# Gate and up products: both parts of x behind the weights' first part, as one operand of 512 columns

## The chip, the cores and the metric

The kernel runs on one core of one Trainium2 chip. The metric is device time in microseconds (us); less is better. Engines are called as the profile calls them: PE (TensorE, matmuls), PEld (its weight loads), DVE (VectorE), ACT (ScalarE), POOL (GpSimd), SP (SyncE, which issues most DMAs).

## The reference, cut to what matters

The model is an encoder of two layers over 256 tokens of 1024 channels. Each layer has a feed-forward part, a group of four mixers, and a second feed-forward part, each between two norms. The feed-forward part is what the change touches:

```
def swiglu(h, w_gate, w_up, w_down):
    return (jax.nn.silu(h @ w_gate) * (h @ w_up)) @ w_down
...
    x = x + 0.5 * rms_norm(swiglu(rms_norm(x, g[0]), gate, up, down), g[1])
```

The gate and up weights are 1024 x 2816, the down weights 2816 x 1024, all float32. There are four such parts in all (two per layer).

## The kernel before

A float32 product is made from matmuls on fp32r operands. Each operand is split in two parts, a first part (hi, a rounded copy made by ACT) and a second part (lo, the rest, made by DVE), and three of the four products of parts are summed: `TERMS = ((0, 0), (0, 1), (1, 0))` in line 253.

Weights come through `Stream.next` (lines 229 to 251). It issues one DMA of 512 KB on SP's queue into one of four raw buffers, then ACT copies hi and DVE subtracts lo into buffers of the pools `w4`, `m4` or `k4`. A raw buffer comes free when DVE's subtraction has read it, and only then is its next DMA issued; a hi or lo buffer comes free when the last matmul that reads it is done.

The 2816 hidden channels are 22 blocks of 128. For a block, `block(fb)` (line 400) computes gate and up: the weights' 128 columns are the stationary operand, the 256 tokens of x are the moving one, and k runs over eight pieces of 128 channels. The two sums, of 256 columns each, lie in the two halves of one PSUM bank, `pg`. Gate (u = 0) takes 24 matmuls, then up (u = 1) takes 24. After that ACT applies Silu to the gate half (tile `h`), DVE multiplies it with the up half, and ACT and DVE split the product into `hT`, hi and lo. `rows` (line 419) then multiplies `hT` with the down weights: moving operands of 512 columns, three matmuls for each half of y and token tile, so 12 matmuls for a block's two token tiles.

The main loop of `ffn` runs block(fb + 1) and then rows(fb), so a block's hT is needed one block later. From block 15 on (`NFB - NEPI`) only the first token tile's rows are done in the loop, 6 matmuls in place of 12; the second tile's are kept for the end, where they cover the norm that joins this part to the next. Blocks 20 and 21 follow each other with no rows between. Block 0, and in three of the four parts blocks 1 and 2 too, go through `half_block` by token tile, which the change leaves as it is but for indices; the first part sends 21 blocks through `block`, the others 19 each.

`pg` has the PSUM tag "d", which has two banks (`PD` = 2). Half blocks, the mixers' projections and the norm's transposes of some tiles use the same two banks. With one bank per block, a block's bank is needed again two blocks later.

`norm_t` (line 275) normalises x and transposes it; its inner `part` (line 299) empties each bank of four transposed pieces with one ACT copy (hi) and one DVE subtraction (lo) of 128 x 512. The four tiles of XT hold hi and lo apart, each with four of the eight pieces.

The order of work on each engine isn't written in the code alone: a scheduler of the framework orders the instructions when the program is built, from priorities in order of the program and a model of their durations. On the chip each engine then takes them in that order, and one that waits holds back those behind it.

Of the kernel before, what the change touches and what calls it, by code (L numbers as in the profile page):

```python
# [9 lines left out]
F32 = mybir.dt.float32  # L10
# [76 lines left out]
# column blocks of w_in in the order in which they are used; -1 marks a column that is not there  # L87
# [18 lines left out]
def tile_encoder(ctx: ExitStack, tc: tile.TileContext, x_in, wffn, win, wout, gains, params, idn, cst, rel, out, dbg=None):  # L106
# [55 lines left out]
    def s1(name, shape=(P, S), dt=F32):  # L162
        return sp.tile(list(shape), dt, tag="s1", bufs=3, name=name)
# [39 lines left out]
    def load_small(l):  # L203
        if l == 0:
            nc.sync.dma_start(out=C, in_=cst)
            # log-sigmoid of the retention's decays: forward, backward
            for i in range(DEPTH):
                o, w = _POFF["rl"]
                nc.sync.dma_start(out=lg[:, i, 0:8], in_=params[i][:, o:o + w])
            act(pair, c_("pair"), AF.Copy)  # L210
            lgr, lgt = lg[:, :, 0:8], lg[:, :, 8:16]
            act(lgt, lgr, AF.Abs)
            act(lgt, lgt, AF.Exp, scale=-1.0)
            act(lgt, lgt, AF.Ln, bias=1.0)
            stt(lgr, lgr, 0.0, lgt, ALU.min, ALU.subtract)
        t = par[l] = sp.tile([P, NPAR], F32, tag="par", bufs=1, name=f"par{l}")
        nc.sync.dma_start(out=t, in_=params[l])
        t = dv[l] = sp.tile([P, 30], F32, tag="dv", bufs=2, name=f"dv{l}")
        ts(t[:, 0:8], p_(l, "mu"), -1.0, ALU.mult, 1.0, ALU.add)
        ts(t[:, 8:16], p_(l, "mu"), 0.5, ALU.mult)  # L220
        ts(t[:, 16:24], par[l][:, _POFF["w0"][0]:_POFF["w0"][0] + 8], 0.5, ALU.mult)
        ts(t[:, 24:26], p_(l, "ka"), 0.5, ALU.mult)
        ts(t[:, 26:28], p_(l, "ka"), -0.5, ALU.mult, 1.0, ALU.add)
        ts(t[:, 28:30], p_(l, "kk"), 512.0, ALU.mult)

# [1 line left out]
    @contextmanager  # L227
    def held(*ins):
        """the instructions issue after these, each on its own engine."""
        with ExitStack() as c:  # L230
            for i in ins:
                c.enter_context(tc.issue_after(i.ins))
            yield
# [37 lines left out]
    def new_xt(l, i):  # L271
        new = m4 if i == 2 else k4
        return [[new([P, 4, S], F32R, name=f"XT{l}_{i}{a}{q}") for q in range(2)] for a in range(2)]

    def norm_t(XT, g, tk, tag, hold=()):
        """The normalised x with its gain, transposed, in two parts: [part][k // 4][d, k % 4, token].
        What it returns issues the transposes."""
# [21 lines left out]
        def part(q):  # L299
            pt = ps.tile([P, 4, P], F32, tag=tag, bufs={"d": PD, "a": PA, "y": PY}[tag], name="pt")  # L300
            for k in range(4):
                T.transpose(pt[:, k, :], xg[:, (q * 4 + k) * P:(q * 4 + k + 1) * P], ident)
            hi = XT[0][q][:, :, tk * P:(tk + 1) * P]
            ends[:] = (act(hi, pt, AF.Copy),
                       V.tensor_tensor(out=XT[1][q][:, :, tk * P:(tk + 1) * P], in0=pt, in1=f(hi), op=ALU.subtract))  # L305
# [3 lines left out]
    def resid(g, yt, tk, half):  # L309
        """x += (1 or 1/2) of the normalised y with its gain."""  # L310
        c = 2.0 if half else 1.0
        st = sp.tile([P, 3], F32, tag="st3", bufs=4, name="st3")
        for h in range(2):
            jk = sp.tile([P, 512], BF16, tag="jk", bufs=1, name="jk")
            act(jk, yt[h], AF.Square, scale=c / 32.0, accum_out=st[:, h:h + 1])
        yg = k4([P, D], name="yg")
        mul(yg[:, 0:512], yt[0], g[:, 0:512])
        stt(st[:, 2:3], st[:, 0:1], c * c * RMS_EPS, st[:, 1:2], ALU.add, ALU.add)
        r = rstd(st[:, 2:3], 1, "r_y")
        mul(yg[:, 512:1024], yt[1], g[:, 512:1024])  # L320
        for h in range(2):
            hs = slice(h * 512, (h + 1) * 512)
            stt(x[tk][h], yg[:, hs], r[:, 0:1], x[tk][h], ALU.mult, ALU.add)
# [4 lines left out]
    def rowgemm(yt, hT, wd, tk, first, last):  # L328
        """y[token, 1024] += hT^T (two parts) @ wd (two parts) for one token tile."""
# [5 lines left out]
    def colgemm_y(dst, w, XT, hold=None):  # L335
        """dst[col, token] = w^T @ XT for one piece of 8 x 128 columns."""
        n = 0
        for k in range(8):
            for a, b in TERMS:
                with tc.issue_after(hold.ins) if hold and n == 0 else nullcontext():  # L340
                    T.matmul(dst, lhsT=w[a][:, k * P:(k + 1) * P], rhs=XT[b][k // 4][:, k % 4, :], start=n == 0, stop=n == 23)  # L341
# [9 lines left out]
    def ffn(hold, l, j, XT, before2, ahead, after, first, last, mix_next):  # L351
        """before2(): what makes XT's second token tile; after(tk, y): what follows a finished token tile."""
# [23 lines left out]
        def half_block(fb, tk, inside=None):  # L376
# [3 lines left out]
            for k in range(8):  # L380
# [3 lines left out]
                for a, b in TERMS:  # L384
                    T.matmul(pg, lhsT=XT[a][k // 4][:, k % 4, tk * P:(tk + 1) * P], rhs=w[b][:, c:c + 256],  # L385
# [14 lines left out]
        def block(fb):  # L400
            wa, wb = ws[fb][:2]
            pg = ps.tile([P, 2, S], F32, tag="d", bufs=PD, name="pg")
            for u in range(2):
                n = 0
                for k in range(8):
                    w, c = (wa, wb)[k // 4], (k % 4) * 256 + u * P
                    for a, b in TERMS:
                        T.matmul(pg[:, u, :], lhsT=w[a][:, c:c + P], rhs=XT[b][k // 4][:, k % 4, :],  # L408
                                 start=n == 0, stop=n == 23, skip_group_check=True)
                        n += 1  # L410
            h = s1("h")
            act(h, pg[:, 0, :], AF.Silu)
            mul(h, h, pg[:, 1, :])
# [5 lines left out]
        def rows(fbs, tk):  # L419
            """y[token, 1024] += h^T wd for some blocks, one half of the columns after the other."""  # L420
# [80 lines left out]
    # ================= mixers =================  # L501
# [4 lines left out]
    def mixers(hold, l, XT, before2, ahead, after):  # L506
# [4 lines left out]
        def vg(before2):  # L511
            """two groups of 256 columns by token, [token, 512] for each token tile."""
# [3 lines left out]
            for n in range(16):  # L516
# [4 lines left out]
                for i, (a, b) in enumerate(TERMS):  # L521
                    T.matmul(pv[tk], lhsT=XT[a][k // 4][:, k % 4, tk * P:(tk + 1) * P],  # L522
# [3 lines left out]
        def vg_y():  # L526
            pv = [ps.tile([P, 512], F32, tag="d", bufs=PD, name=f"pvh{i}") for i in range(2)]
            pvh.extend(pv)
            for j in range(4):
                w = st.next()  # L530
                for tk in range(2):
                    for k in (2 * j, 2 * j + 1):
                        for i, (a, b) in enumerate(TERMS):
                            T.matmul(pv[tk], lhsT=XT[a][k // 4][:, k % 4, tk * P:(tk + 1) * P],  # L534
# [43 lines left out]
        def headsum(dst, a):  # L578
            """sums over each head's channels by token: [token, tile, head]."""
# [5 lines left out]
        def headspread(dst, r):  # L585
            """[token, tile, head] spread over each head's channels: [channel, pair, token]."""
# [6 lines left out]
        # kk's norm over each head's channels (the sum scaled by 2^20, the root by 2^10)  # L593
# [4 lines left out]
        # mLSTM gates: the input gate, the log-sigmoid of the forget gate, heads on partitions  # L598
# [5 lines left out]
        # the running maximum in two parts, on two groups of partitions  # L604
# [6 lines left out]
        # decay and in-context rate; the backward direction is kept in reversed time  # L611
# [55 lines left out]
        # half of kk  # L667
# [9 lines left out]
        # operands of the chunks: alpha, r; beta, k for the first pair of heads, k, beta for the second  # L677
# [29 lines left out]
        def finish(o_, gate, m, scale=None):  # L707
            """rms over each head, gate, transpose, split: o_, gate are [token, tile, ...256]."""
# [24 lines left out]
        def rwkv():  # L733
# [21 lines left out]
            # v by time (both directions), beta and k by time, A_ak V  # L755
# [22 lines left out]
            # bonus: the sum over channels of r * (kd_f + kd_b) * r_k, spread over the head's channels; gate  # L778
# [17 lines left out]
            # out = xc rstd (ln_w gate) + (ln_b + bonus) gate  # L796
# [4 lines left out]
            # (I - A)^-1: 16 x 16 blocks one to a partition, then two merges  # L801
# [42 lines left out]
            def spread(name, src):  # L844
                """16 x 16 blocks on partitions -> [(head, 32-block, row), system, column in the 32-block]."""
# [49 lines left out]
            # the off-diagonal 32 x 32 blocks  # L895
# [35 lines left out]
            # the chain over the chunks; O^T[(head, v), pair, token] gathers both directions  # L931
# [55 lines left out]
            # group norm over each head's channels, bonus, gate  # L987
# [26 lines left out]
        # the other mixers: shared tiles, then their parts as generators of instructions  # L1014
# [59 lines left out]
        def mlstm():  # L1074
            yield 0.0
            # weights exp(c_s - M_t) of the causal tiles: [s, head, t]
# [65 lines left out]
            # decays: exp(lg_f (t - s)) above, exp(lg_b (s - t)) below  # L1142
# [69 lines left out]
        def mix(a, b, ratio):  # L1212
            """b runs beside a: for each unit of a's time on PE, ratio units of b's."""
# [20 lines left out]
        # output projection: its sums begin before the last mixer is done  # L1234
# [63 lines left out]
    # PE's clock rises under load: zeros, until the first data is there  # L1298
# [44 lines left out]
def _layout(inputs):  # L1343
# [3 lines left out]
    # [.., 1024, 128 n] -> [.., n, p, k, 128]  # L1347
# [31 lines left out]
    def chan(a):  # [depth, .., 256] -> [depth, p, (.., 2)]  # L1379
# [46 lines left out]
```

## Time and profile before

| what | us |
|---|---|
| median of three runs (1179.52 to 1182.47) | 1182.34 |
| the profiled execution, first to last instruction (its span) | 1177.6 |
| PE busy in it | 1140.7 (97%) |
| PEld busy | 1033.4 (88%) |
| DVE busy | 738.0 (63%) |
| ACT busy | 588.0 (50%) |
| POOL busy | 95.4 (8%) |

The profile tells of its execution's own time only the span. The median of the timed runs is 4.7 us above it, the fastest 1.9 us; that much lies around the first and the last instruction, or between executions.

Busy time of PE is the union of its matmuls, which overlap, so a matmul's duration isn't what it costs; the distance between the starts of two that follow each other is. In the chain of waits, times of PE are counted from the end of the matmul before, some 0.17 us after the start in the timeline.

### The profile page before, as it was taken

Reading aid. Unit: us, or ns where it says so; the run is one execution under the profiler, and the core shown is the slowest. Engines: PE = TensorE matmul, PEld = TensorE weight load, DVE = VectorE, ACT = ScalarE, POOL = GpSimd, SP = SyncE. Lnnn points to the kernel's source line nnn. Section 1 sums busy time; section 2 is a strip of 40 time slices with the busy share of each in tenths; the row PEclk is TensorE's granted clock in tenths of the full one; section 3 lists DMA queues with packets and bytes.
Section 4 is the critical chain, followed back from the end, with each engine's and each line's share of the span. In section 5 each row is a group of like instructions: output and inputs, shape, how many; then the busy total and the mean of one; then the engine's idle time right before and its main releaser. Section 6 shows DMA issues by size and latency. Waiting matters only on the chain.

```text
span 1177.6 us, 22471 instructions
## 1 busy us (share of the span) xinstructions
PE 1140.7 (97%) x9332; PEld 1033.4 (88%) x9332; DVE 738.0 (63%) x1171; ACT 588.0 (50%) x979; POOL 95.4 (8%) x159
## 2 busy tenths in 40 slices
PE   8999999979999999999999999999799999999997
PEld 7999999878888789999989999989778888999997
DVE  6655455798775855555675555467897668554543
ACT  5564445657334644444554444457573356444441
POOL 0000000243100100000000000013431001000000
PEclk8999999988999999999999999999899999999999
DMA  7655564412341675556536555535124326665550
GB/s 278 230 186 190 186 214 162 143 37 90 123 140 35 197 231 179 187 185 224 197 123 204 189 182 194 197 126 179 40 80 146 110 91 197 203 192 180 191 182 36
DMA packets 53094, 190.12 MB, mean 161 GB/s; under 512 B 6144, under 2 KB 6272, under 8 KB 52992
## 3 DMA queue, kind: packets, MB, share of 16 engines
q1 hardware_dynamic: 50976, 181.61, 47.3%
q10 hardware_dynamic: 2016, 7.08, 1.8%
q8 instruction: 73, 1.20, 0.4%
q14 instruction: 29, 0.24, 0.1%
HBM read 187.62 MB, written 1.05 MB: 160 GB/s over the span
## 4 chain that ended last, share of the span: by engine, by line
PE 71%; DVE 11%; DMA 8%; ACT 4%; issue 3%; POOL 1%; DVEq 0%; POOLq 0%; SPq 0%; ACTq 0%
PE pg L408 32%; PE y L424 16%; PE pz L341 10%; DMA f_raw<-in_wffn_dram 6%; DVE f_lo L121 3%; ACT f_hi L142 2%; PE pgh L385 1%; PE pvg L522 1%; PE pgr L743 1%; DMA rl<-in_rel_dram 1%; DVE x L139 1%; PE pvh L534 1%; DVE xg L121 1%; POOL r_n L121 1%; PE pom L1123 1%
## 5 line engine op out<-in xcount | busy, mean ns | idle before, releaser
L121 DVE TENSOR_TENSOR f_lo<-f_raw,f_hi 128x1024 fp32r<-128x1024 f32 (+1 forms) x280 | 321.4, 1162 | 278.1 <-ACT f_hi L142 274.0
L408 PE MATMUL pg<-XT,f_hi 128*128 128x256 f32 x2496 | 452.3, 283 | 0.0
L142 ACT ACTIVATE f_hi<-f_raw 128x1024 fp32r<-128x1024 f32 (+1 forms) x280 | 278.0, 1008 | 258.6 <-DMA f_raw<-in_wffn_dram 171.1
L408 PEld LDWEIGHTS pg<-XT,f_hi 128*128 128x128 f32 x2496 | 393.8, 192 | 5.5
L408 PE MATMUL pg<-XT,f_lo 128*128 128x256 f32 x1248 | 353.2, 283 | 0.0
L408 PEld LDWEIGHTS pg<-XT,f_lo 128*128 128x128 f32 x1248 | 239.3, 192 | 0.0
L424 PE MATMUL y<-f_hi,hT 128*128 128x512 f32 x704 | 233.0, 393 | 2.6 <-DVE hT L121 1.5
L424 PEld LDWEIGHTS y<-f_hi,hT 128*128 128x128 f32 x704 | 132.1, 188 | 30.8 <-DVE hT L121 2.9
L341 PE MATMUL pz<-XT,i_hi 128*128 128x256 f32 x704 | 145.9, 301 | 1.2 <-ACT zp L142 1.2
L424 PE MATMUL y<-f_lo,hT 128*128 128x512 f32 x352 | 138.0, 392 | 0.0
L341 PEld LDWEIGHTS pz<-XT,i_hi 128*128 128x128 f32 x704 | 113.6, 196 | 13.1 <-issue 6.0
L341 PE MATMUL pz<-XT,i_lo 128*128 128x256 f32 x352 | 102.7, 292 | 0.9 <-DVE i_lo L121 0.9
L121 DVE TENSOR_TENSOR i_lo<-i_raw,i_hi 128x1024 fp32r<-128x1024 f32 (+1 forms) x68 | 75.8, 1126 | 20.3 <-ACT i_hi L142 19.5
L142 ACT ACTIVATE i_hi<-i_raw 128x1024 fp32r<-128x1024 f32 (+1 forms) x68 | 64.1, 954 | 47.9 <-PE pz L341 18.1
L142 ACT ACTIVATE hT<-h 128x256 fp32r<-128x256 f32 x78 | 32.5, 417 | 88.1 <-DVE h L121 88.0
L424 PEld LDWEIGHTS y<-f_lo,hT 128*128 128x128 f32 x352 | 66.4, 189 | 10.9
L341 PEld LDWEIGHTS pz<-XT,i_lo 128*128 128x128 f32 x352 | 69.1, 196 | 2.7 <-DVE i_lo L121 1.4
L121 POOL TENSOR_TENSOR r_y<-st,nhalf 128x1 f32<-128x1 f32 x12 | 6.5, 540 | 776.5 <-DVE st L139 776.5
L385 PE MATMUL pgh<-f_hi,XT 128*128 128x256 f32 x320 | 62.9, 292 | 0.9 <-DVE XT L305 0.6
L385 PEld LDWEIGHTS pgh<-f_hi,XT 128*128 128x128 f32 x320 | 52.4, 196 | 2.3 <-DVE XT L305 1.3
L417 DVE TENSOR_TENSOR hT<-h,hT 128x256 fp32r<-128x256 f32 x78 | 33.0, 423 | 29.8 <-ACT hT L142 29.8
L385 PE MATMUL pgh<-f_lo,XT 128*128 128x256 f32 x160 | 46.4, 290 | 1.8 <-DVE f_lo L121 1.6
(290 smaller groups left out, 1252.8 us busy)
## 6 DMA issues: line engine op xcount, KB each, us to landing
f_raw<-in_wffn_dram SPq DMA_DIRECT2D x264, 512.0 KB, 4.3
i_raw<-in_win_dram SPq DMA_DIRECT2D x60, 512.0 KB, 4.1
o_raw<-in_wout_dram SPq DMA_DIRECT2D x16, 512.0 KB, 3.8
gain<-in_gains_dram ACTq DMA_DIRECT2D x12, 512.0 KB, 5.5
x<-in_x_dram SPq DMA_DIRECT2D x4, 256.0 KB, 7.0
out_dram<-x SPq DMA_DIRECT2D x4, 256.0 KB, 2.0
rl<-in_rel_dram ACTq DMA_DIRECT2D x2, 384.0 KB, 5.3
C<-in_cst_dram SPq DMA_DIRECT2D x1, 573.0 KB, 7.9
```

The source lines that it names most:

```text
L121: eng.tensor_tensor(out=out, in0=a, in1=b, op=op)
L139: V.scalar_tensor_tensor(out=out, in0=a, scalar=s, in1=b, op0=op0, op1=op1)
L142: return A.activation(out, a, f, **kw)
L341: T.matmul(dst, lhsT=w[a][:, k * P:(k + 1) * P], rhs=XT[b][k // 4][:, k % 4, :], start=n == 0, stop=n == 23)
L385: T.matmul(pg, lhsT=XT[a][k // 4][:, k % 4, tk * P:(tk + 1) * P], rhs=w[b][:, c:c + 256], start=n == 0, stop=n == 23)
L408: T.matmul(pg[:, u, :], lhsT=w[a][:, c:c + P], rhs=XT[b][k // 4][:, k % 4, :], start=n == 0, stop=n == 23, skip_group_check=True)
L417: V.tensor_tensor(out=hT[:, 1, :], in0=h, in1=f(hT[:, 0, :]), op=ALU.subtract))
L424: ins = T.matmul(y[tk][h], lhsT=hts[fb][:, a, tk * P:(tk + 1) * P], rhs=ws[fb][2][b][:, h * 512:(h + 1) * 512], start=fb == 0 and i == 0, ...
L522: T.matmul(pv[tk], lhsT=XT[a][k // 4][:, k % 4, tk * P:(tk + 1) * P], rhs=w[b][:, (k % 2) * 512:(k % 2 + 1) * 512], start=k == 0 and i == ...
L534: T.matmul(pv[tk], lhsT=XT[a][k // 4][:, k % 4, tk * P:(tk + 1) * P], rhs=w[b][:, (k % 2) * 512:(k % 2 + 1) * 512], start=k == 0 and i == ...
L743: T.matmul(pg[:, n, :], lhsT=bk[d][hs, p, n, :, :].rearrange("p a t -> p (a t)"), rhs=ar[d][hs, 4 * p + n, :, :].rearrange("p a t -> p (a ...
L1123: T.matmul(po[half[c], h, :], lhsT=wf[d][sk][:, h, o0 + 64 * c:o0 + 64 * c + 64], rhs=v1[:, sk, h, :], start=h == 0 and sk == sks[0], stop ...
```

## The change

The tiles of XT hold both parts side by side: four tiles, each with two of the eight pieces, and for each piece hi's 256 columns and then lo's. In `block`, gate and up get a bank each. For each piece k, one matmul of 512 columns passes hi and lo of x behind the weights' hi, into both halves of the bank; a second, of 256 columns, passes hi of x behind the weights' lo, into the first half. When the bank is emptied, ACT copies the second half to SBUF, DVE adds the first half, and for gate ACT applies Silu to that sum in SBUF. DVE then multiplies gate and up in SBUF. Tag "s1" gets a fourth buffer. `part` empties its bank in two pieces of 256 columns each, since the tiles are cut in another way; other readers of XT only have other indices. The products summed are the same three.

```
     def new_xt(l, i):
         new = m4 if i == 2 else k4
-        return [[new([P, 4, S], F32R, name=f"XT{l}_{i}{a}{q}") for q in range(2)] for a in range(2)]
+        return [new([P, 2, 2, S], F32R, name=f"XT{l}_{i}{q}") for q in range(4)]
+
+    def xt(XT, k, a):
+        return XT[k // 2][:, k % 2, a, :]
+
+    def xt2(XT, k):
+        return XT[k // 2][:, k % 2, :, :]
...
-            hi = XT[0][q][:, :, tk * P:(tk + 1) * P]
-            ends[:] = (act(hi, pt, AF.Copy),
-                       V.tensor_tensor(out=XT[1][q][:, :, tk * P:(tk + 1) * P], in0=pt, in1=f(hi), op=ALU.subtract))
+            for j in range(2):
+                t = XT[2 * q + j]
+                hi, src = t[:, :, 0, tk * P:(tk + 1) * P], pt[:, 2 * j:2 * j + 2, :]
+                ends[:] = (act(hi, src, AF.Copy),
+                           V.tensor_tensor(out=t[:, :, 1, tk * P:(tk + 1) * P], in0=src, in1=f(hi), op=ALU.subtract))
...
         def block(fb):
             wa, wb = ws[fb][:2]
-            pg = ps.tile([P, 2, S], F32, tag="d", bufs=PD, name="pg")
+            gu = []
             for u in range(2):
-                n = 0
+                pg = ps.tile([P, 2, S], F32, tag="d", bufs=PD, name="pg")
                 for k in range(8):
                     w, c = (wa, wb)[k // 4], (k % 4) * 256 + u * P
-                    for a, b in TERMS:
-                        T.matmul(pg[:, u, :], lhsT=w[a][:, c:c + P], rhs=XT[b][k // 4][:, k % 4, :],
-                                 start=n == 0, stop=n == 23, skip_group_check=True)
-                        n += 1
-            h = s1("h")
-            act(h, pg[:, 0, :], AF.Silu)
-            mul(h, h, pg[:, 1, :])
+                    T.matmul(pg, lhsT=w[0][:, c:c + P], rhs=xt2(XT, k), start=k == 0, stop=False, skip_group_check=True)
+                    T.matmul(pg[:, 0, :], lhsT=w[1][:, c:c + P], rhs=xt(XT, k, 0), start=False, stop=k == 7, skip_group_check=True)
+                t = s1("gu")
+                act(t, pg[:, 1, :], AF.Copy)
+                add(t, pg[:, 0, :], t)
+                if u == 0:
+                    act(t, t, AF.Silu)
+                gu.append(t)
+            h = gu[0]
+            mul(h, h, gu[1])
```

## Rows read from the trace of the kernel before

**Rows 1.** The page's first part: busy time, share of the span and instructions of each engine.

```profile
PE 1140.7 (97%) x9332; PEld 1033.4 (88%) x9332; DVE 738.0 (63%) x1171; ACT 588.0 (50%) x979; POOL 95.4 (8%) x159
```

**Rows 2.** The chain of waits in order of time, in the first feed-forward part: start us, us, what.

```profile
91.22 5.75 PE pg L408 x48
96.97 2.75 PE y L424 x12
99.72 5.75 PE pg L408 x48
...
179.28 11.51 PE pg L408 x96
190.79 10.91 PE y L424 x48
```

**Rows 3.** Busy time of each engine in a stretch of the main loop: stretch, its length, then PE, PEld, DVE, ACT and POOL busy with their instructions, granted clock, DMA share, GB/s.

```profile
57.00:140.00 83.00, 83.00 (x592) 78.42 (x592) 43.48 (x57) 42.18 (x56) 0.00 (x0) 1.00 0.57 189
```

**Rows 4.** The costliest groups of the page: the matmuls of `block`, and the copies of `hT` (one for each call of `block`).

```profile
L408 PE MATMUL pg<-XT,f_hi 128*128 128x256 f32 x2496 | 452.3, 283 | 0.0
L408 PE MATMUL pg<-XT,f_lo 128*128 128x256 f32 x1248 | 353.2, 283 | 0.0
L142 ACT ACTIVATE hT<-h 128x256 fp32r<-128x256 f32 x78 | 32.5, 417 | 88.1 <-DVE h L121 88.0
```

**Rows 5.** The timeline of PE at the end of a block, and at the start of the next: start us, us from the first start to the last end, what.

```profile
105.19 0.28 PE L408 MATMUL pg<-XT,f_lo 128*128 128x256 f32 x1
105.31 0.40 PE L424 MATMUL y<-f_hi,hT 128*128 128x512 f32 x1
105.54 0.40 PE L424 MATMUL y<-f_lo,hT 128*128 128x512 f32 x1
105.78 0.62 PE L424 MATMUL y<-f_hi,hT 128*128 128x512 f32 x2
...
107.83 0.39 PE L424 MATMUL y<-f_hi,hT 128*128 128x512 f32 x1
108.05 0.40 PE L408 MATMUL pg<-XT,f_hi 128*128 128x256 f32 x2
108.28 0.28 PE L408 MATMUL pg<-XT,f_lo 128*128 128x256 f32 x1
```

**Rows 6.** The timelines of ACT and DVE in the same round of the main loop; in brackets the idle time before and what ended it.

```profile
102.44 1.06 ACT L142 ACTIVATE f_hi<-f_raw 128x1024 fp32r<-128x1024 f32 x1 [2.40 <-DMA f_raw<-in_wffn_dram]
106.40 0.36 ACT L142 ACTIVATE h<-pg 128x256 f32<-128x256 f32 x1
106.53 1.23 DVE L121 TENSOR_TENSOR f_lo<-f_raw,f_hi 128x1024 fp32r<-128x1024 f32 x1 [0.21 <-ACT f_hi L142]
107.67 0.41 DVE L121 TENSOR_TENSOR h<-h,pg 128x256 f32<-128x256 f32 x1
108.57 0.42 DVE L417 TENSOR_TENSOR hT<-h,hT 128x256 fp32r<-128x256 f32 x1 [0.48 <-ACT hT L142]
```

**Rows 7.** The timelines of ACT, DVE and PE near the end of the first feed-forward part.

```profile
161.22 0.33 ACTq L263 DMA_DIRECT2D gain<-in_gains_dram  x1
171.66 2.01 ACT L142 ACTIVATE f_hi<-f_raw 128x1024 fp32r<-128x1024 f32 x2 [6.22 <-DMA f_raw<-in_wffn_dram]
179.72 2.01 ACT L142 ACTIVATE f_hi<-f_raw 128x1024 fp32r<-128x1024 f32 x2 [3.82 <-DMA f_raw<-in_wffn_dram]
181.63 0.36 ACT L142 ACTIVATE h<-pg 128x256 f32<-128x256 f32 x1
...
180.81 2.36 DVE L121 TENSOR_TENSOR f_lo<-f_raw,f_hi 128x1024 fp32r<-128x1024 f32 x2 [3.89 <-ACT f_hi L142]
183.09 0.41 DVE L121 TENSOR_TENSOR h<-h,pg 128x256 f32<-128x256 f32 x1
...
179.11 0.40 PE L408 MATMUL pg<-XT,f_hi 128*128 128x256 f32 x2
```

**Rows 8.** The same two events, DVE's product and the start of the block after it on PE, near the ends of the second, third and fourth part.

```profile
573.15 0.41 DVE L121 TENSOR_TENSOR h<-h,pg 128x256 f32<-128x256 f32 x1
569.18 0.40 PE L408 MATMUL pg<-XT,f_hi 128*128 128x256 f32 x2
...
766.22 0.41 DVE L121 TENSOR_TENSOR h<-h,pg 128x256 f32<-128x256 f32 x1
761.27 0.40 PE L408 MATMUL pg<-XT,f_hi 128*128 128x256 f32 x2
...
1149.37 0.42 DVE L121 TENSOR_TENSOR h<-h,pg 128x256 f32<-128x256 f32 x1
1146.35 0.40 PE L408 MATMUL pg<-XT,f_hi 128*128 128x256 f32 x2
```

**Rows 9.** The timelines of ACT and DVE after the last block of the first part, which ends on PE at 190.79 in rows 2.

```profile
190.82 0.38 ACT L142 ACTIVATE h<-pg 128x256 f32<-128x256 f32 x1 [0.36 <-PE pg L408]
192.15 0.42 DVE L417 TENSOR_TENSOR hT<-h,hT 128x256 fp32r<-128x256 f32 x1 [0.48 <-ACT hT L142]
```

**Rows 10.** The timelines of ACT and DVE where a norm's transposes are emptied into XT, and of PE's first matmul that reads them.

```profile
202.17 1.09 ACT L142 ACTIVATE XT<-pt 128x512 fp32r<-128x512 f32 x2 [1.58 <-PE pt L302]
202.80 1.29 DVE L305 TENSOR_TENSOR XT<-pt,XT 128x512 fp32r<-128x512 f32 x2 [2.45 <-ACT XT L142]
212.16 0.50 PE L522 MATMUL pvg<-i_hi,XT 128*128 128x512 f32 x1 [0.25 <-ACT XT L142]
```

More of the change, by code (lines that the diff above doesn't have):

```diff
@@ L162, in s1 @@
     def s1(name, shape=(P, S), dt=F32):
-        return sp.tile(list(shape), dt, tag="s1", bufs=3, name=name)
+        return sp.tile(list(shape), dt, tag="s1", bufs=4, name=name)
     def a1(name, shape=(P, S), dt=F32):
@@ L340, in colgemm_y @@
                 with tc.issue_after(hold.ins) if hold and n == 0 else nullcontext():
-                    T.matmul(dst, lhsT=w[a][:, k * P:(k + 1) * P], rhs=XT[b][k // 4][:, k % 4, :], start=n == 0, stop=n == 23)
+                    T.matmul(dst, lhsT=w[a][:, k * P:(k + 1) * P], rhs=xt(XT, k, b), start=n == 0, stop=n == 23)
                 n += 1
@@ L384, in half_block @@
                 for a, b in TERMS:
-                    T.matmul(pg, lhsT=XT[a][k // 4][:, k % 4, tk * P:(tk + 1) * P], rhs=w[b][:, c:c + 256],
+                    T.matmul(pg, lhsT=xt(XT, k, a)[:, tk * P:(tk + 1) * P], rhs=w[b][:, c:c + 256],
                              start=n == 0, stop=n == 23)
@@ L521, in vg @@
                 for i, (a, b) in enumerate(TERMS):
-                    T.matmul(pv[tk], lhsT=XT[a][k // 4][:, k % 4, tk * P:(tk + 1) * P],
+                    T.matmul(pv[tk], lhsT=xt(XT, k, a)[:, tk * P:(tk + 1) * P],
                              rhs=w[b][:, (k % 2) * 512:(k % 2 + 1) * 512], start=k == 0 and i == 0, stop=k == 7 and i == 2)
@@ L533, in vg_y @@
                         for i, (a, b) in enumerate(TERMS):
-                            T.matmul(pv[tk], lhsT=XT[a][k // 4][:, k % 4, tk * P:(tk + 1) * P],
+                            T.matmul(pv[tk], lhsT=xt(XT, k, a)[:, tk * P:(tk + 1) * P],
                                      rhs=w[b][:, (k % 2) * 512:(k % 2 + 1) * 512], start=k == 0 and i == 0, stop=k == 7 and i == 2)
```

## The prediction

> **What bounds the kernel now.** I read the page's busy times first: PE is busy 97% of the span, DVE 63%, ACT 50% [rows 1]. An average hides where the others bind, so the chain of waits in order of time comes next. In the main loop of a feed-forward part it is PE alone: 48 matmuls of a block in 5.75 us, 12 of the rows in 2.75, and again, one round in 8.50 [rows 2]. The stretches say the same: PE busy 83.00 of 83.00 us at a granted clock of 1.00, which is the higher of its two levels, with ACT and DVE about half busy [rows 3]. So a change of PE's work in a block changes the time directly, as long as what empties the banks keeps up. The timelines of ACT and DVE show whether it does: well in the main loop [rows 6], late near the end of each part [rows 7, 8].
>
> **The change part by part.**
>
> *The matmuls.* `block` is called 78 times (78 copies of hT; 2496 + 1248 = 3744 matmuls are 48 for each call) [rows 4]. A call loses 48 matmuls of 256 columns and gets 16 of 512 and 16 of 256. That is 12,288 columns both times: what can be saved is what a matmul costs beside its columns. Two blocks on end take 11.51 us for 96 matmuls of 256, 0.120 each; 48 matmuls of 512 on end take 10.91, 0.227 each, which is less than twice 0.120 [rows 2]. So there is something to save, 0.013 for each pair of 256 that becomes one 512. But the new stream alternates, and no stretch of the trace does. Its nearest rows are the seams. After 256s the first 512 takes 0.23 (105.31 to 105.54) and the second 0.24; after 512s the first two of 256 take 0.23 together, 0.115 each [rows 5]. A pair of one 512 and one 256 thus costs between 0.227 + 0.115 = 0.342 and 0.24 + 0.12 = 0.36. I take 0.347, the seams' 0.23 and 0.117, because in the new stream every matmul stands at a seam. Sixteen pairs are 5.55 us against 5.75: 0.20 saved, times 78 is 15.6. The ends are 5.47 (0.28, in all 21.8 saved) and 5.76 (0.01 lost, in all 0.8 lost).
>
> At 2.4 GHz, the level granted here, 256 columns are 0.1067 us and 512 are 0.2133, so the rows show 0.013 to 0.014 beside the columns [rows 2, 3]. The Trainium skill, TensorE: Matmul & The Clock Gate, section "Wait — 56ns, not 53.3ns?", gives a fixed cost of about 2.5 ns for each warm matmul. By that an estimate would be 16 matmuls fewer times 2.5 ns, 0.04 us a block and 3 us in all; the trace doesn't agree with it, five times as much is shown, in a stream that loads new weights for every matmul.
>
> *Emptying the bank.* Before, a call has Silu (0.36 on ACT), the product (0.41 on DVE) and the split of hT [rows 6]. Now it has two copies of 128 x 256 (as Silu, 0.36 each), two additions (as the product, 0.41 each), Silu and the product: 0.72 more on ACT, 0.82 more on DVE. In the main loop ACT is busy 42.18 of 83.00, 4.3 a round, and DVE 43.48, 4.5 [rows 3]; they go to 5.0 and 5.3 of a round of 8.30. PE covers that. If the cover were gone it would be some 1.5 us a round, in series.
>
> *The banks.* This is the wait that the change adds. A block takes both banks, so gate's bank must be empty when the next block starts, up's when the next block is half done; before, a bank had a whole block more. What is queued behind a waiting matmul is all of PE. The up half's last reader is now DVE's addition, which stands where the product stood. In the main loop the product of the block that ended at 105.3 is done at 107.67 + 0.41 = 108.08; the next up sum starts at 108.05 + 2.87 = 110.92 [rows 5, 6]. That is 2.8 us of room: no wait. Gate's sum ends in the middle of the block, at 102.4, and even behind the split that waits for a DMA until 102.44 its addition has some 2.5 us of room [rows 6].
>
> Near the end of a part the room is gone. The rows there last half as long, and the loads of the norms' gains come in [rows 7]. In the first part ACT sits idle 6.22 and 3.82 us in front of splits that wait for their DMA, and the product stands behind two of them on DVE: it ends at 183.50, while the middle of the next block is at 179.11 + 2.87 = 181.98. That is 1.5 us late [rows 7]. Before, nobody waited for it. The same reckoning gives 573.56 - 572.05 = 1.5 in the second part, 766.63 - 764.14 = 2.5 in the third and 1149.79 - 1149.22 = 0.6 in the fourth [rows 8]. PE would wait that long once in each part, since each wait moves all later blocks: 6.1 us. The blocks there are also 0.2 shorter while the DMAs keep their pace, so I add 0.3 for each part, 1.2. Bounds: nothing, if the scheduler puts the copies ahead of those splits; and 2.87 more in each part, if gate's emptying is queued as late as up's.
>
> *After the last block.* Before, Silu starts at 190.82 and hT is done at 192.57, and the rows that need it come 12 matmuls after 190.62, the end of the block in the timeline, at 193.37 [rows 2, 9]. The new chain has one more link, 0.41 and a hand-over, against 0.8 of room. I take 0.5 for all four parts; between nothing and 2.
>
> *The norms.* For each token tile two copies of 0.57 and two subtractions of 0.69 become four and four; a 256-column one takes 0.36 to 0.41 [rows 6, 10]. The first piece is ready some 0.4 sooner, the last some 0.3 later. PE waits 0.25 for the first of them in the row shown [rows 10]. Twelve times between -0.4 and +0.3, and only where PE waits: I take 0, with 2 to either side.
>
> *Sum.* -15.6 + 6.1 + 1.2 + 0.5 = -7.8 on the profiled span of 1177.6, so 1169.8. The median of the timed runs is 4.7 above that span, and nothing in the change touches what lies around it: 1174.5.
>
> **The rivals.**
>
> *All of it arrives.* ACT's order puts the copies ahead of the late splits, and no bank is waited for: -15.6 + 0.5, so 1167. For it: the new instructions come earlier in the program than the splits of later blocks. Against it: two splits stand ahead of Silu in the rows that are late now [rows 7].
>
> *Gate's bank is late too.* One mechanism, from one point: if near the end of a part the copy of the gate half is queued behind the split that waits for its DMA, PE waits at the start of the block, half a block (2.87) earlier than I reckoned. That is 11.5 more over four parts: -7.8 + 11.5 = +3.7, 1186, slower than before. It decides wherever the DMA lands later than the middle of a block. For it: the split at 171.66 starts when its block is over. Against it: a copy that is ready earlier in the scheduler's model goes first, and there the gains' DMAs may not delay the splits as they do on the chip.
>
> *The alternating stream saves nothing.* Weights are loaded anew before each matmul, PEld is busy 88% [rows 1], and a 256 between two 512s may pay for both seams: 0.36 a pair. Then +0.8 + 7.8 = +8.6, 1191. A saving of only 0.04 a block gives -3.1 + 7.8, 1187; that is what the Trainium skill's 2.5 ns would come to. Against both: 0.227 for a 512 in a long run, where each also has its own weights [rows 2].
>
> *Half and half.* The pair costs 0.353 and the banks as forecast: -8 + 7.8, no change, 1182.
>
> **How the numbers follow.** The forecast (1169 to 1180) has 0.50, all of it 0.20, gate's bank 0.13, nothing saved in the stream 0.09, half and half 0.08. A measurement of this kernel can tell 0.3% from no change, 3.5 us: under 1178.8 is faster, over 1185.9 slower. Faster are nine tenths of the forecast and all of the first rival, 0.65; the same are the rest of the forecast, half and half and some of gate's bank, 0.18; slower 0.17. The range leaves out one in ten on either side: below, the bound of 21.8 saved with half of the waits is 1164; above, gate's bank at 1186.
>
> **What would show it.** In the chain, blocks of 5.55 and rounds of 8.30 with PE alone in the main loop show the stream right; 5.75 shows the third rival. Matmuls of 512 at 0.23 and of 256 at 0.117 in the timeline show the seams. Near the end of each part PE should wait on DVE's addition, at the middle of a block, for 1 to 3 us once; a wait at the start of a block shows the second rival, none shows the first. ACT and DVE should gain some 56 and 64 us of busy time, as 78 times 0.72 and 0.82. I am wrong if PE waits in the main loop, or if the mixers, which the change hardly touches, move by more than 2 us.

## The result and the profile after

The changed kernel takes 1175.18 us (median of 8 runs, 1168.35 to 1176.76) against 1182.4 for the kernel before in the same comparison (8 runs): a ratio of 0.9945, with a 95% interval of 0.9922 to 0.9968. The forecast was 1174.5. The experiments below show that this agreement is half luck: three terms of the sum were off, and their errors cancel in part. Two more comparisons of the same kernel gave 1.0007 and 0.9975, neither of them clear of no change by itself. Two of the executions counted below, both of the kernel before (1191.31 and 1192.51), were slow ones, which the ratios leave out and the last column of the table keeps; that moves its values by some 0.1.

The profiled span is 1174.0. The page of the changed kernel, first part and four groups (columns as in [rows 1] and [rows 4]):

```profile
PE 1133.7 (97%) x8084; PEld 966.0 (82%) x8084; DVE 799.9 (68%) x1351; ACT 641.9 (55%) x1159; POOL 92.3 (8%) x159
...
L418 PE MATMUL pg<-XT,f_hi 128*128 128x512 f32 x1248 | 444.4, 398 | 3.5 <-DVE gu L121 3.4
...
L419 PE MATMUL pg<-XT,f_lo 128*128 128x256 f32 x1248 | 350.0, 280 | 0.0
...
L121 DVE TENSOR_TENSOR gu<-pg,gu 128x256 f32<-128x256 f32 x156 | 65.2, 418 | 15.2 <-ACT gu L142 15.2
...
L142 ACT ACTIVATE gu<-pg 128x256 f32<-128x256 f32 x156 | 57.6, 369 | 19.2 <-PE pg L419 18.6
```

ACT has gained 53.9 us and DVE 61.9 [rows 1]; 56 and 64 were forecast. There are two new things to see in these lines: PE now sits idle 3.4 us in front of block's first kind of matmul, until DVE's addition (`gu`) has emptied a bank; in [rows 4] that column is 0.0. And a mean of 398 ns says nothing of the cost of a 512, since matmuls overlap; that is read from the distance of starts.

The chain of waits in order of time, third feed-forward part (start us, us, what). The matmuls of `block` stand in it one by one and are left out here:

```profile
644.07 2.75 PE y L438 x12
...
652.45 2.75 PE y L438 x12
...
660.84 2.75 PE y L438 x12
```

A round, one block and its rows, is 8.39, where it was 8.50 [rows 2] and 8.30 was forecast. So a block takes 5.64, not 5.55. The timeline of PE shows why (start us, us from first start to last end, what):

```profile
98.28 0.40 PE L418 MATMUL pg<-XT,f_hi 128*128 128x512 f32 x1
98.51 0.28 PE L419 MATMUL pg<-XT,f_lo 128*128 128x256 f32 x1
98.63 0.40 PE L418 MATMUL pg<-XT,f_hi 128*128 128x512 f32 x1
98.87 0.28 PE L419 MATMUL pg<-XT,f_lo 128*128 128x256 f32 x1
98.99 0.40 PE L418 MATMUL pg<-XT,f_hi 128*128 128x512 f32 x1
```

Two pairs take 98.99 - 98.28 = 0.71, so a pair takes 0.353 over sixteen of them. A 512 takes some 0.236 until the next start, a 256 takes 0.117.

Near the end of the first part, the timelines of ACT, DVE and PE (in brackets the idle time before, and what ended it):

```profile
160.80 1.06 ACT L142 ACTIVATE f_hi<-f_raw 128x1024 fp32r<-128x1024 f32 x1 [2.01 <-DMA f_raw<-in_wffn_dram]
...
161.76 0.36 ACT L142 ACTIVATE gu<-pg 128x256 f32<-128x256 f32 x1
...
161.89 1.23 DVE L121 TENSOR_TENSOR f_lo<-f_raw,f_hi 128x1024 fp32r<-128x1024 f32 x1 [2.64 <-ACT f_hi L142]
163.03 0.42 DVE L121 TENSOR_TENSOR gu<-pg,gu 128x256 f32<-128x256 f32 x1
...
163.51 0.50 PE L418 MATMUL pg<-XT,f_hi 128*128 128x512 f32 x1 [1.03 <-DVE gu L121]
163.84 0.28 PE L419 MATMUL pg<-XT,f_lo 128*128 128x256 f32 x1
```

The block before began at 155.28, so its gate sum was complete some 2.8 later, near 158.1. ACT then sat idle for 2.01, but its next instruction in order was a split of weights (the copy that makes hi), whose DMA landed only at 160.80. Gate's copy stood behind that split, and its addition behind the split's second half on DVE. PE waited 1.03, at the start of a block, for gate's bank. Such a wait costs more than its idle time. The matmul in front of it starts at 162.08, where 0.22 to the next start is usual, so 1.21 are lost; the next start is 0.33 away, where 0.236 is usual. That is 1.30 in all, 0.27 more than the 1.03 shown. The other waits for banks over 0.15 us stand in the second part: 0.69 and 0.95 at the start of a block, and 0.48 and 0.22 in the middle of one, for up's.

### The profile page after: what moved, and what is told of

It is laid out like the page before. It is cut to its first block, busy times and chain, and to the rows that moved or that the text cites. A ratio compares the mean times of both kernels' runs of the same rounds, so it can differ in the third digit from the quotient of the medians.

```text
span 1174.0 us, 20406 instructions
## 1 busy us (share of the span) xinstructions
PE 1133.7 (97%) x8084; PEld 966.0 (82%) x8084; DVE 799.9 (68%) x1351; ACT 641.9 (55%) x1159; POOL 92.3 (8%) x159
## 3 DMA queue, kind: packets, MB, share of 16 engines
q8 instruction: 63, 1.03, 0.4%
## 5 line engine op out<-in xcount | busy, mean ns | idle before, releaser
L418 PE MATMUL pg<-XT,f_hi 128*128 128x512 f32 x1248 | 444.4, 398 | 3.5 <-DVE gu L121 3.4
L418 PEld LDWEIGHTS pg<-XT,f_hi 128*128 128x128 f32 x1248 | 234.4, 188 | 62.7 <-DVE gu L121 6.4
L419 PEld LDWEIGHTS pg<-XT,f_lo 128*128 128x128 f32 x1248 | 235.6, 189 | 2.7
L142 ACT ACTIVATE hT<-gu 128x256 fp32r<-128x256 f32 x78 | 32.6, 418 | 126.3 <-DVE gu L121 126.3
L121 DVE TENSOR_TENSOR gu<-pg,gu 128x256 f32<-128x256 f32 x156 | 65.2, 418 | 15.2 <-ACT gu L142 15.2
L438 PEld LDWEIGHTS y<-f_lo,hT 128*128 128x128 f32 x352 | 66.1, 188 | 11.5 <-DVE f_lo L121 0.8
L142 ACT ACTIVATE gu<-pg 128x256 f32<-128x256 f32 x156 | 57.6, 369 | 19.2 <-PE pg L419 18.6
L431 DVE TENSOR_TENSOR hT<-gu,hT 128x256 fp32r<-128x256 f32 x78 | 33.1, 425 | 34.9 <-ACT hT L142 34.9
```

The costliest lines, as they stand in the source:

```text
L121: eng.tensor_tensor(out=out, in0=a, in1=b, op=op)
L142: return A.activation(out, a, f, **kw)
L418: T.matmul(pg, lhsT=w[0][:, c:c + P], rhs=xt2(XT, k), start=k == 0, stop=False, skip_group_check=True)
L419: T.matmul(pg[:, 0, :], lhsT=w[1][:, c:c + P], rhs=xt(XT, k, 0), start=False, stop=k == 7, skip_group_check=True)
L431: V.tensor_tensor(out=hT[:, 1, :], in0=h, in1=f(hT[:, 0, :]), op=ALU.subtract))
L438: ins = T.matmul(y[tk][h], lhsT=hts[fb][:, a, tk * P:(tk + 1) * P], rhs=ws[fb][2][b][:, h * 512:(h + 1) * 512], start=fb == 0 and i == 0, ...
```

## The experiments

Each comparison has its own runs of the kernel before, and ratios with 95% intervals are against those. The last column is explained under "What had not been expected": the mean of all executions, moved to one granted clock. It compares executions of several chips, and the kernel before has 1181.2, 1181.0 and 1182.0 in its three comparisons. The first result had 8 more runs of the kernel before, whose clocks aren't on record; they aren't among the 81.

| kernel | median | ratio to before | at clock 0.984 |
|---|---|---|---|
| before, three comparisons (81 runs) | 1181.03, 1179.77, 1181.36 | | 1181.4 |
| the change (32 runs) | 1175.18, 1179.47, 1176.03 | 0.9945 [0.9922, 0.9968], 1.0007 [0.9979, 1.0035], 0.9975 [0.9947, 1.0003] | 1176.4 |
| layout alone (24) | 1177.63, 1176.02 | 0.9962 [0.9932, 0.9993], 0.9955 [0.9926, 0.9984] | 1177.5 |
| fourth s1 buffer alone (12) | 1179.78 | 1.0008 [0.9984, 1.0032] | 1181.0 |
| change, grouped (12) | 1175.12 | 0.996 [0.9935, 0.9985] | 1176.6 |
| change, three banks (12) | 1174.45 | 0.9954 [0.9928, 0.9981] | 1174.8 |
| change, stream of 256 (6) | 1191.23 | 1.0087 [1.0063, 1.0112] | 1194.5 |
| change, gate first (6) | 1168.38 | 0.9911 [0.9883, 0.9939] | 1167.7 |
| stream of 256, gate first (12) | 1177.03 | 0.9968 [0.9938, 0.9999] | 1176.9 |
| grouped and gate first (12) | 1161.22, 1160.44 | 0.9853 [0.9822, 0.9883], 0.9833 [0.9788, 0.9878] | 1161.5 |

**The seams.** The eight 512s of a half sum come first, then its eight 256s:

```
                 for k in range(8):
                     w, c = (wa, wb)[k // 4], (k % 4) * 256 + u * P
                     T.matmul(pg, lhsT=w[0][:, c:c + P], rhs=xt2(XT, k), ...)
+                for k in range(8):
+                    w, c = (wa, wb)[k // 4], (k % 4) * 256 + u * P
                     T.matmul(pg[:, 0, :], lhsT=w[1][:, c:c + P], rhs=xt(XT, k, 0), ...)
```

> The change with one edit: in each half sum all eight matmuls of 512 columns come first, then the eight of 256, so that two seams are left of sixteen. The changed kernel's round of the main loop was 8.39 us, a pair 0.353. If the seams cost the difference to 0.227 + 0.120, the first few 512s of a run still pay (0.233, 0.236 and 0.228 to 0.232 in the kernel before), and a block gets some 0.05 us shorter: rounds of 8.33, 4 us in all, about 0.991 of the kernel before. If the 0.353 belongs to the pair wherever it stands (its weight loads), rounds stay at 8.39 and the ratio at 0.9945.

The chain of waits of the grouped kernel:

```profile
643.69 1.81 PE pg L418 x8
645.50 0.95 PE pg L421 x8
646.46 1.84 PE pg L418 x8
648.30 0.95 PE pg L421 x8
649.25 2.75 PE y L440 x12
652.00 1.81 PE pg L418 x8
```

Its group of 512s:

```profile
L418 PE MATMUL pg<-XT,f_hi 128*128 128x512 f32 x1248 | 313.5, 393 | 7.7 <-DVE gu L121 7.6
```

A block is now 1.81 + 0.95 + 1.84 + 0.95 = 5.55 and a round 8.31, which is what had been forecast for the change itself. So the seams are what keeps the changed kernel at 5.64. But the time doesn't move (1176.6 against 1176.4 at equal clock): PE waits 7.6 us for banks, in place of 3.4, 4.9 and 4.5 in the three profiles of the change. The faster stream meets the same late DMAs sooner, and the wait takes back what the stream gives.

**Is it the bank, or the emptying that is late?** A third bank for the half sums:

```
-                pg = ps.tile([P, 2, S], F32, tag="d", bufs=PD, name="pg")
+                tag = "d" if fb <= NPRO else ("d", "o", "d")[(2 * fb + u) % 3]
+                pg = ps.tile([P, 2, S], F32, tag=tag, bufs=PD if tag == "d" else 1, name="pg")
```

> The change with one edit: from the second call of block in each part on, the half sums go round three PSUM banks in place of two (the third is the bank that only the transposes of half blocks and the mixers use). If the waits of PE on DVE's addition (3.5 us on the page, at nine places near the ends of the first two parts) are for the bank alone, they go and the time falls by 3 to 4.5 us, about 0.991 of the kernel before. If the late DMAs stand behind them, PE waits for weights or for hT in the same places and the time stays within 1 us.

The groups of that kernel's block and rows:

```profile
L419 PE MATMUL pg<-XT,f_hi 128*128 128x512 f32 x1248 | 443.7, 398 | 0.5 <-DVE gu L121 0.5
...
L439 PE MATMUL y<-f_hi,hT 128*128 128x512 f32 x704 | 235.6, 396 | 8.3 <-ACT hT L142 6.8 <-DVE hT L121 1.4
```

The waits for banks fall to 0.5, and 8.3 us stand in front of `rows`, which wait for hT. A late gate sum holds up Silu, the product and hT too; a bank more only lets PE run on to the next place that needs the same result. At equal clock it gains 1.6, with standard errors of 0.9 and 0.4: not told apart from nothing.

**The stream put back.** The new emptying and banks, with the matmuls of 256 as before:

```
-                    T.matmul(pg, lhsT=w[0][:, c:c + P], rhs=xt2(XT, k), start=k == 0, ...)
+                    for e in range(2):
+                        T.matmul(pg[:, e, :], lhsT=w[0][:, c:c + P], rhs=xt(XT, k, e), start=k == 0 and e == 0, ...)
```

> The change with its matmuls of 512 columns split into two of 256 again (48 of 256 a block, as before); banks, emptying and layout are those of the change. If the whole gain is the stream's 0.113 us a block, it is lost: rounds of 8.50, some 9 us over the changed kernel and, with waits for banks of 1 to 4 us, 1.000 to 1.004 of the kernel before. If the two banks and the early emptying of gate bring something by themselves, it stays under 0.998.

```profile
L419 PE MATMUL pg<-XT,f_hi 128*128 128x256 f32 x2496 | 456.3, 284 | 11.0 <-DVE gu L121 10.6
```

That is the group of its first kind of matmul: 10.6 us of waits for banks, of which some stand in the main loops of the first and third part (1.00 at 69.88, 0.71 at 684.14), where the profile of the change above has none over 0.15. The kernel takes 1191.23, a ratio of 1.0087, more than was expected. Each kernel gets its own order from the scheduler, and this one's is worse (with gate put first the same matmuls take 1177.03, below), so the difference to the change (18.1 at equal clock) isn't the price of the stream alone.

**The layout alone.** The changed XT, emptied in two pieces, and the fourth s1 buffer, with `block` as before:

```
         def block(fb):
...
                     for a, b in TERMS:
-                        T.matmul(pg[:, u, :], lhsT=w[a][:, c:c + P], rhs=XT[b][k // 4][:, k % 4, :],
+                        T.matmul(pg[:, u, :], lhsT=w[a][:, c:c + P], rhs=xt(XT, k, b),
```

> The kernel before with the change's layout of XT and the emptying of the transposes in two pieces alone; block is as before but for indices, tag s1 has four buffers. By the prediction this is worth nothing: 0.998 to 1.002 of the kernel before. If the 1.6 us that the first mixers took longer in the changed kernel's trace come from here, the ratio is 1.001 to 1.003 and the mixers of this trace are longer by as much.

> The layout alone a second time (0.9962 [0.9932, 0.9993] before). If the layout with its emptying in two pieces is worth some 4 us, 0.994 to 0.998 again; if that was the spread between batches, 0.999 to 1.002.

Two comparisons on two chips say the same, 0.9962 and 0.9955. Where it comes from can be read at the starts of the parts. The group of the rows in the kernel before:

```profile
L424 PE MATMUL y<-f_hi,hT 128*128 128x512 f32 x704 | 233.0, 393 | 2.6 <-DVE hT L121 1.5 <-ACT hT L142 0.9
```

The same group with the layout alone:

```profile
L434 PE MATMUL y<-f_hi,hT 128*128 128x512 f32 x704 | 233.0, 393 | 0.4 <-DVE hT L121 0.3
```

A half block that follows a norm, in the second part, in PE's timeline of the kernel before:

```profile
411.12 0.39 PE L385 MATMUL pgh<-f_lo,XT 128*128 128x256 f32 x1 [0.79 <-DVE f_lo L121]
```

Its counterpart in PE's timeline with the layout alone:

```profile
402.76 0.51 PE L395 MATMUL pgh<-f_hi,XT 128*128 128x256 f32 x2 [0.31 <-DVE XT L315]
```

The wait of 0.79 stands in the fourth part too, and both are 0.31 with the layout; the 0.25 of [rows 10], which the kernel before has in both layers, is gone. That is 2.2 in front of the rows, 2 x 0.48 and 2 x 0.25, 3.7 of idle time, where the two kernels differ by 3.9 at equal clock. It isn't a full account: the second profile of the layout has 0.7 in front of the rows, and both have a wait of 1.66 for XT at the start of the first part, where the kernel before has 0.56 and 0.25.

**The buffer.** The kernel before with four s1 buffers, nothing else:

```
-        return sp.tile(list(shape), dt, tag="s1", bufs=3, name=name)
+        return sp.tile(list(shape), dt, tag="s1", bufs=4, name=name)
```

> The kernel before with the fourth buffer of tag s1 alone. The layout run (with this buffer) came to 0.9962 of the kernel before, where nothing was forecast. If the buffer is what helps (half blocks keep their product in it), this gives 0.995 to 0.998 too, and the waits of PE for hT at the start of the second and fourth part (0.70, 1.00 and 0.54 in the kernel before) are gone; if it is the layout with its emptying in two pieces, 0.999 to 1.001 and the waits stay.

The ratio is 1.0008, and waits of 0.79 for `f_lo` stand at 409.02 and 987.05 as before. In front of the rows there are 1.7, partly in other places than before (1.00 at 434.05, 0.67 at 625.75), so up to 0.9 of the 2.2 above may be spread or the buffer's. The gain itself isn't the buffer's: it is XT's tiles and their emptying. Which of these two does it, the cut of the tiles or the two pieces, was not tried apart.

**Gate first.** The splits of weights that arrive during a block are kept behind the copy and the addition of an earlier gate half, each on its own engine. `st.hold[i]` names the instructions after which the split of the stream's i-th piece issues:

```
         def fetch_ab(fb):
...
+            for i in range(2):
+                if fb - 2 in gates:
+                    st.hold[st.i + i] = gates[fb - 2]
...
         def fetch_d(fb):
...
+            if fb - 1 in gates:
+                st.hold[st.i] = gates[fb - 1]
...
-                act(t, pg[:, 1, :], AF.Copy)
-                add(t, pg[:, 0, :], t)
+                ins = act(t, pg[:, 1, :], AF.Copy), V.tensor_tensor(out=t, in0=pg[:, 0, :], in1=t, op=ALU.add)
+                if u == 0:
+                    gates[fb] = ins
```

> The change with one edit of the order: the splits of later weights on ACT and DVE are issued after the copy and the addition that empty the gate bank (splits of gate and up weights behind those of two blocks before, of down weights behind those of the block before). If gate's bank is late because it is queued behind a split that waits for its DMA, PE's waits on DVE's addition (3.4 us on the page of the change) go to under 1 us and the time falls by 2 to 4 us, 0.991 to 0.993 of the kernel before. If the DMAs' lateness is the cause, held splits only make them later: PE waits for hT or weights as with three banks, and the time is that of the change or up to 3 us more.

The timelines of ACT and DVE at the place where the changed kernel waited:

```profile
158.07 0.38 ACT L142 ACTIVATE gu<-pg 128x256 f32<-128x256 f32 x1 [0.70 <-PE pg L424]
158.35 1.05 ACT L142 ACTIVATE f_hi<-f_raw 128x1024 fp32r<-128x1024 f32 x1
...
158.49 0.42 DVE L426 TENSOR_TENSOR gu<-pg,gu 128x256 f32<-128x256 f32 x1 [0.66 <-ACT gu L142]
```

The group of the 512s:

```profile
L423 PE MATMUL pg<-XT,f_hi 128*128 128x512 f32 x1248 | 443.9, 399 | 0.0
```

Gate's copy now waits for PE, not for a DMA, and PE waits for no bank (0.0). The ratio is 0.9911, and the fall is larger than the 2 to 4 us expected: 8.7 at equal clock, 9.5 against the change's runs in the same comparison. This is the second rival's mechanism, and its cause is the order on ACT and DVE, not the amount of work: the instructions are the same.

**Grouped and gate first.** Both edits together:

> Both edits together, grouped matmuls and gate emptied first. The grouped run had rounds of 8.31 against 8.39 (some 6 us over 78 blocks) but waits for banks of 6.6 against 3.4 us and the same time as the change. If the waits were a matter of order, both gains stand: 0.987 to 0.990 of the kernel before, better than either. If they are the DMAs, 0.993 to 0.996 again.

> Grouped matmuls and gate first again, on the chip of this batch: 0.983 to 0.988 of the kernel before if the gain doesn't hang on a batch's DMAs, since no bank was waited for in its main loops; 0.988 to 0.994 if it does.

(On the grouped kernel's page the 6.6 of the first expectation is 7.6.) With the wait gone the seams pay: 6.2 us at equal clock below gate first, where 0.08 a round times 78 is 6.2. Both comparisons put this kernel at 0.985 and 0.983 of the kernel before. It beats both kernels.

**The stream of 256 with gate first**, which prices the stream without a bad order:

> The stream of 256s in the change's banks and emptying (1.0087 before), with gate emptied ahead of later splits as in the gate-first run (0.9911). If the erratic waits of up to 1.4 us in the rounds of the first and third part were a matter of the order on ACT and DVE, they go, rounds are 8.50 throughout, and the ratio is 0.997 to 1.001; the distance to the gate-first run is then the stream alone, some 9 us. If the emptying costs time by itself, it stays over 1.004.

```profile
89.01 2.75 PE y L445 x12
97.51 2.75 PE y L445 x12
106.01 2.75 PE y L445 x12
```

In its chain the rounds are 8.50 and undisturbed. At equal clock it takes 1176.9, as the layout alone does (1177.5): the two copies and two additions for each block cost nothing that these runs can tell once they are in a good order. And 1176.9 - 1167.7 = 9.2 is what the stream of 512 brings; 0.11 a round times 78 is 8.6. The traces say the same: from the start of the third part's first matmul of `block` to the start of its last it takes 152.01 here and 149.77 with gate first, 0.118 for each of 19 blocks.

**The change again**, two more comparisons of the unaltered changed kernel:

> The change itself, unedited, for a second profile and more times beside the other kernels of this batch: 0.992 to 0.997 of the kernel before, rounds of 8.39 and the same instructions in the same order, so that what differs between its two traces is the spread of the mixers and of DMAs, expected within 4 us of span.

> The change itself a third time, since two batches gave 0.9945 [0.9922, 0.9968] and 1.0007 [0.9979, 1.0035] for the same instructions in the same order. If what differs is the landing of DMAs, on which the waits for gate's bank hang, the ratio lies between the two, 0.994 to 1.001, with rounds of 8.39 in the trace and waits for banks of 3 to 6 us.

They gave 1.0007 and 0.9975, with the same instructions in the same order on every engine; the first is outside the range expected. The first of the two profiled executions has its waits for banks at 33.17, 164.92, 541.39, 549.36, 559.97 and 741.91, 4.9 us in all; the second has 4.5, and the first result's had none in the third part. When a weight DMA lands differs from one execution to the next, and the waits with it: the split at 730.82, a block ahead of the wait at 741.91, waits 2.58 for its DMA, and the same split 1.00 in the first result's trace (732.48).

## Why the prediction was right, and where only its sum was

**Time and direction.** Faster was likeliest, and 0.9945 says faster. Over all 32 executions at equal clock the change is worth 1181.4 - 1176.4 = 5.0 us, 0.4%; the forecast was 7.8. The two later comparisons give 3.8 and 4.2 by themselves, and without the correction for the clock the means differ by 3.4 (1180.8 and 1177.4). That 1175.18 came so close to 1174.5 is thus also luck of the first comparison, whose executions are some 4 us faster at equal clock than the later ones.

**The matmuls, mis-sized.** "I take 0.347, the seams' 0.23 and 0.117." The 256 is 0.117; the 512 behind it is 0.236, not 0.23, and [rows 5] had both (105.31 to 105.54, then 0.24). The pair is 0.353, some way above the middle of the bounds 0.342 and 0.36, and a block saves 0.11, so 8.6 in all by the rounds (9.2 by the times), not 15.6. The fourth rival had this stream, with 8 saved. The Trainium skill, TensorE: Matmul & The Clock Gate, section "Wait — 56ns, not 53.3ns?", gives a warm matmul a fixed cost of about 2.5 ns; an estimate by that is 3 us for the 16 matmuls fewer in each block. The trace doesn't agree with it: the measured 8.6 is well above.

**The banks, misplaced.** "Gate's sum ends in the middle of the block [...] its addition has some 2.5 us of room" holds in the main loop, and I didn't carry it to the end of a part, where I let only up's half be late. The runs show the second rival's mechanism in its place: waits at the start of a block, for gate's bank, behind a split whose DMA is late. The place that I forecast, up's bank in the middle of a block, has 0.48 and 0.22 of the 3.4. The size is not the rival's 7.3 + 11.5: the DMAs land late in only some of the rounds. Gate first removes the waits and takes 8.7 us off the changed kernel at equal clock. Of these, the groups show 3.4 to 4.9 for the bank and 1.5 less in front of the rows (2.2 there, 0.7 with gate first). The rest is the 0.27 that each wait costs beside its idle time, and a few starts late by so little that no idle time shows. Counted from start to start it is all there: from the first matmul of `block` in a part to the last, the four parts together take 617.5 with gate first and 625.1, 625.6 and 626.6 in the three profiles of the change, 7.6 to 9.1 more. So the forecast's 7.3 was near the right size, but by luck: another bank, another place in the block, and more waits, each shorter. In the later two profiles one even stands early in the first part (0.66 at 33.17, 0.28 at 32.02), where no wait was forecast.

**After the last block.** 0.5 was forecast in all. The rows at 583.82, behind the second part's last block, waited 0.66 for hT, where the kernel before has 0.24; the other parts have no such wait.

**The norms, missed.** "I take 0, with 2 to either side." The layout is worth 3.9 us at equal clock (3.2 and 5.1 in its two comparisons), nearly as much as the net gain of 5.0. I had asked only about the row in [rows 10], and not which other waits end at a part's start; the rows' group of the kernel before (2.6 us until hT) and the 0.79 of the half blocks would have shown some 3.7 us that an earlier XT could touch. Why the new tiles and pieces shorten these waits is not shown.

**The sum.** At equal clock: -3.9 for the layout, -9.2 for the stream, +8.7 for the order, and -0.6 for what the emptying adds in a good order, make -5.0 (each is the difference of two kernels of the table, so they add up by construction; standard errors are about 0.5 to 0.8 each, and kernels of different comparisons can differ by another 1 or so). In the forecast they were 0, -15.6, +7.3 and +0.5. The stream brought 6.4 less than forecast, and the layout's 3.9 made up for the greater part of that.

**What lay around the span.** I took 4.7 us from the median. In the runs of the change the time is 1.7 above the span each time (1175.67 and 1174.0), and so it is in the later runs of the kernel before (1178.32 and 1176.6). So the profiled execution of before ran some 3 us below its median, and that was spread between executions, not time outside the span.

## What to carry to other kernels

When a change makes a buffer come free later, follow every emptying instruction back in its engine's order to the one ahead of it that waits for a DMA: the engine's busy share (ACT 55%, DVE 68% here) says nothing of that, and naming the order was worth 8.7 us, where a third bank's 1.6 could not be told from nothing. Here a faster stream paid only once those waits were gone: grouping like with like brought nothing before, and 6.2 us after. Price a wait on PE from start to start, since its idle time shows only part of it. And price a "layout only" edit by the waits of the trace that end on the tile it touches.

## What had not been expected

**An alternating stream costs more than its parts.** In long runs of their own kind a 512 takes 0.227 and a 256 0.120 [rows 2], together 0.347; alternating they take 0.353, and grouped in eights 0.347 again (5.55 / 16).

**One program, one order, and a spread of over 1%, which follows the granted clock.** The 12 executions of the second comparison of the change run from 1172.19 to 1188.69. Each execution has a mean granted clock; over the table's 209 executions, taken within each kernel and comparison, time falls by 8.8 us for 0.01 of it (correlation -0.81). The table's last column moves each mean to 0.984 by that slope: for the second comparison of the change, whose mean clock was 0.9811, this takes 2.6 us off 1179.8. It leaves 1173.2, 1177.2 and 1177.8 for the three comparisons, so some difference stays. Busy times by stretch show where the clock differs. Three stretches of the execution profiled in the change's second comparison (columns as in [rows 3]; the granted clock is third from the end):

```profile
258.00:261.00 3.00, 0.00 (x0) 0.00 (x0) 2.84 (x7) 0.89 (x3) 0.00 (x0) 0.78 0.00 0
...
267.00:270.00 3.00, 3.00 (x15) 2.78 (x14) 2.10 (x3) 2.02 (x3) 0.66 (x1) 0.51 0.41 153
270.00:273.00 3.00, 3.00 (x29) 2.75 (x27) 2.13 (x4) 1.13 (x2) 1.18 (x2) 1.00 0.61 175
```

And of the one profiled in its third comparison:

```profile
258.00:261.00 3.00, 0.00 (x0) 0.00 (x0) 2.91 (x5) 0.41 (x1) 0.80 (x1) 0.72 0.00 0
...
270.00:273.00 3.00, 3.00 (x18) 2.77 (x17) 0.57 (x2) 0.11 (x1) 0.00 (x0) 0.50 0.60 175
273.00:276.00 3.00, 3.00 (x14) 2.75 (x13) 2.54 (x5) 1.41 (x3) 1.88 (x2) 0.50 0.29 64
276.00:279.00 3.00, 3.00 (x24) 2.68 (x23) 2.63 (x5) 1.31 (x5) 0.00 (x0) 0.94 0.56 164
```

In the mixers of both layers PE stands idle for over 5 us while DVE works, and there the clock falls from 1.00 to 0.50, that is from 2.4 to 1.2 GHz. PE is busy again from about 262 on, at half speed: until 270 in the one execution, past 276 in the other, with 14 to 18 matmuls in 3 us in place of 24 to 29. The same stretch of the second layer differs in the same way. The spans differ by 7.6 us (1171.1 and 1178.7), and the two mixers by 8.4 (435.9 and 444.3, from the start of the first mixer's value projection to the next part's first block). So the mixers do move by more than the 2 us at which I had said I would be wrong, between executions of one and the same kernel. What decides when the clock rises again, no run here shows.
